# Row maxima of a 64 MB matrix: tail rows turned by TensorE and reduced by GpSimd, other load sizes, and a moved store

## The chip, the cores and the metric

The kernel runs on one core of one Trainium2 chip. The metric is the device time of one execution in microseconds (us), as the median of several runs. TensorE is written PE in the profile, VectorE DVE, ScalarE ACT, GpSimd POOL and SyncE SP.

## The reference

The input x has shape (32, 512, 1024) in 32-bit floats, which is 67.1 MB. The output is the maximum over the last axis, shape (32, 512):

```python
def reference(x):
    return np.max(x, axis=-1).astype(np.float32)
```

Seen by the kernel, x is a matrix of 16384 rows with 1024 columns, and one number is wanted for each row.

## The kernel before

The rows are spread over the 128 partitions, so each partition holds 128 rows of 1024 columns. In what follows "a row" is one such row in every partition: 128 rows of x, 512 KB. The rows come in two blocks. The first has 112 rows in 15 loads, from 14 rows down to 3, the second 16 rows in 11 loads of two rows and one. In a block of S rows, partition p holds the S rows from p times S on, so each partition reads one piece of consecutive memory per load, and its results leave as one piece as well.

The loop of lines 41 to 55 does three things. For each load, SP issues a DMA from x into a ring of 46 rows in SBUF (line 49; a load that would pass the end of the ring starts at its beginning again, line 47). For each load, VectorE takes the maximum over the columns of all its rows in a single reduction into columns of the tile `res` (line 50). At the end of each block, ACT issues the store of the block's columns of `res` (line 54).

No order is written out by hand. The framework gives each engine its instructions in the order of the loop and adds waits on semaphores. A reduction waits for its load. A load waits for the reductions of the rows whose place in the ring it takes. The DMAs of both queues, SP's and ACT's, take eight semaphores in turn, and a DMA that takes a semaphore again waits for the landing of the DMA that had it before. TensorE, and apart from four start-up constants GpSimd, do nothing.

Of the kernel before, what the change touches and what calls it, by code (L numbers as in the profile page):

```python
# [1 line left out]

# [4 lines left out]


F32 = mybir.dt.float32

BLOCKS = [
    [14, 14, 12, 11, 9, 8, 8, 7, 6, 5, 4, 4, 4, 3, 3],
    [2, 2, 2, 2, 2, 1, 1, 1, 1, 1, 1],
]
RING = 46


@with_exitstack  # L20
def kernel(
    ctx: ExitStack,
    tc: tile.TileContext,
    x: bass.AP,
    out: bass.AP,
):
    nc = tc.nc
    P = 128
    X = mybir.AxisListType.X

    xf = x.flatten_outer_dims()
    N, D = xf.shape
    I = N // P
    of = out.flatten_outer_dims()

    once = ctx.enter_context(tc.tile_pool(name="once", bufs=1))
    ring = once.tile([P, RING, D], F32)
    res = once.tile([P, I], F32)

    at = first = 0  # L40
    for loads in BLOCKS:
        S = sum(loads)
        xb = xf[first * P:(first + S) * P, :].rearrange("(p i) d -> p i d", p=P)
        b = 0
        for g in loads:
            if at + g > RING:
                at = 0
            xc = ring[:, at:at + g, :]
            nc.sync.dma_start(out=xc, in_=xb[:, b:b + g, :])  # L49
            nc.vector.reduce_max(out=res[:, first + b:first + b + g], in_=xc, axis=X)  # L50
            at += g
            b += g
        dst = bass.AP(tensor=of.tensor, offset=of.offset + first * P, ap=[[S, P], [1, S]])
        nc.scalar.dma_start(out=dst, in_=res[:, first:first + S])
        first += S
    assert first == I


# [1 line left out]
_INS = ['x']  # L60
_OUTS = [((32, 512), 'float32')]


# [23 lines left out]
```

## Time and profile before

| | |
|---|---|
| Median of 9 runs | 165.09 us (165.04 to 165.26) |
| The profiled execution | 165.26 us, of which the span is 163.5 us |
| VectorE busy | 138.5 us, 26 reductions |
| Loads on SP's queue | 26 DMAs, 67.11 MB, 96.3% of the span's DMA time |
| Stores on ACT's queue | 2 DMAs, 0.07 MB, 0.2% |
| VectorE idle ahead of a load | 22.5 us in four waits, the longest 20.3 us, at the start |

The span runs from the first to the last instruction of the program in one profiled execution. The page gives busy times for each engine, the span in 40 slices with the busy share in tenths, the DMA queues, the chain of work that ended last, and groups of equal instructions with their mean duration and the idle time just ahead of them. Other answers of the trace give the chain in order of time and, for each engine or queue, what it waited for.

### The profile page before, as it was taken

What the parts mean: (1) busy time and instruction counts of PE and PEld (TensorE: products, weight loads), DVE (VectorE), ACT (ScalarE), POOL (GpSimd) and SP (SyncE); (2) the same over time, 40 slices, a digit from 0 to 9 for tenths busy, and PEclk for the clock granted to TensorE, in tenths of its full rate; (3) what the DMA queues carried; (4) which work ended last, traced back from release to release, by engine and by line L of the source; (5) the groups of instructions that cost most, each with busy time, mean ns of one, the idle gap of its engine ahead of it and who ended that gap; (6) DMA issues with size and microseconds to landing.
All of it is one profiled execution on the core that took longest, in us unless ns stands there. A gap on an engine that the chain in (4) does not pass through costs nothing.

```text
span 163.5 us, 109 instructions
## 1 busy us (share of the span) xinstructions
DVE 138.5 (85%) x26; POOL 0.2 (0%) x4
## 2 busy tenths in 40 slices
DVE  0000099968999999999999999999999999999994
POOL 0000000000000000000000000000000000000000
DMA  6999999999899897999999999999999999999980
GB/s 224 449 449 449 449 449 449 449 405 397 385 445 485 353 518 332 433 433 489 425 393 489 401 442 442 399 425 436 418 425 425 433 416 422 423 420 417 406 337 2
DMA packets 4032, 67.18 MB, mean 411 GB/s; under 512 B 704, under 2 KB 704, under 8 KB 1472
## 3 DMA queue, kind: packets, MB, share of 16 engines
q1 hardware_dynamic: 3744, 67.11, 96.3%
q10 hardware_dynamic: 288, 0.07, 0.2%
HBM read 67.11 MB, written 0.07 MB: 411 GB/s over the span
## 4 chain that ended last, share of the span: by engine, by line
DMA 57%; DVE 40%; DVEq 1%; SPq 0%; issue 0%
DMA ring<-in_x_dram 57%; DVE res L50 40%; DVEq L82 1%; SPq L49 0%
## 5 line engine op out<-in xcount | busy, mean ns | idle before, releaser
L50 DVE TENSOR_REDUCE res<-ring 128x1 f32<-128x1024 f32 (+11 forms) x26 | 138.5, 5398 | 22.5 <-DMA ring<-in_x_dram 22.5
L71 POOL MEMSET const-bfloat16-1.0<- 128x1 bf16 x1 | 0.1, 101 | 0.0
L71 POOL MEMSET const-uint8-127<- 128x1 uint8 x1 | 0.1, 101 | 0.0
L71 POOL MEMSET const-float32-0.0<- 128x1 f32 x1 | 0.1, 98 | 0.2 <-issue 0.2
L71 POOL MEMSET const-float32-1.0<- 128x1 f32 x1 | 0.1, 98 | 0.0
## 6 DMA issues: line engine op xcount, KB each, us to landing
ring<-in_x_dram SPq DMA_DIRECT2D x2, 7168.0 KB, 27.8
ring<-in_x_dram SPq DMA_DIRECT2D x2, 4096.0 KB, 31.6
ring<-in_x_dram SPq DMA_DIRECT2D x1, 6144.0 KB, 50.1
ring<-in_x_dram SPq DMA_DIRECT2D x3, 2048.0 KB, 36.8
ring<-in_x_dram SPq DMA_DIRECT2D x1, 5632.0 KB, 29.6
ring<-in_x_dram SPq DMA_DIRECT2D x5, 1024.0 KB, 24.6
ring<-in_x_dram SPq DMA_DIRECT2D x1, 4608.0 KB, 23.6
ring<-in_x_dram SPq DMA_DIRECT2D x1, 3584.0 KB, 38.3
```

What stands on the lines that cost most here:

```text
L50: nc.vector.reduce_max(out=res[:, first + b:first + b + g], in_=xc, axis=X)
L71: nc = _bacc.Bacc("TRN2", target_bir_lowering=False, num_devices=1)
L82: with _tile.TileContext(nc) as tc:
```

## The change

The change has five parts.

1. The loads: the first block's 112 rows come in 10 loads (15, 15, 15, 13, 13, 11, 9, 9, 6, 6), the second block's first 15 rows in 10 (3, 3, 2 and seven single rows).
2. The last row comes in two loads of 512 columns, the second into a tile of its own, `tail`. VectorE writes the first half's maximum into the column of `tail` just ahead of the second half and then reduces 513 columns. With these there are 22 loads.
3. The first block's store is issued after both loops and waits for the reduction of the last full row, the 20th load's. The second block's store follows on the same queue.
4. One row of the 9th load, three of the 10th and one of the 13th are not reduced by VectorE. For each, TensorE transposes the eight squares of 128 by 128 into PSUM (`turn`), ACT copies the 128x1024 result to SBUF, and GpSimd takes the maximum over the 128 partitions with `partition_all_reduce`, which writes it to every partition. TensorE then turns the first partition's 1024 numbers back in eight pieces (`back`), so that each partition holds the eight maxima of its row's eight column groups, and VectorE reduces these eight into `res`. These merging reductions stand behind the reductions of the 10th, 16th and 19th load.
5. VectorE builds an identity matrix at the start, in eight small instructions, and its instructions and TensorE's are held in a written order by `in_turn`.

On TensorE the order is: turn and way back of the 9th load's row; three turns and the first way back of the 10th load's rows; the turn of the 13th load's row; and then the remaining three ways back. GpSimd also gets one instruction ahead of the first all-reduce, which selects its library, and ACT one that loads its function table.

The core of the diff:

```diff
 BLOCKS = [
-    [14, 14, 12, 11, 9, 8, 8, 7, 6, 5, 4, 4, 4, 3, 3],
-    [2, 2, 2, 2, 2, 1, 1, 1, 1, 1, 1],
+    [15, 15, 15, 13, 13, 11, 9, 9, 6, 6],
+    [3, 3, 2, 1, 1, 1, 1, 1, 1, 1],
 ]
 RING = 46
+TENSOR = {
+    8: [("turn", 8, 0), ("back", 8, 0)],
+    9: [("turn", 9, 0), ("turn", 9, 1), ("turn", 9, 2), ("back", 9, 0)],
+    12: [("turn", 12, 0), ("back", 9, 1), ("back", 9, 2), ("back", 12, 0)],
+}
+BY_GPSIMD = {8: 1, 9: 3, 12: 1}
+MERGE = {9: 8, 15: 9, 18: 12}
...
+    turned = ctx.enter_context(tc.tile_pool(name="turned", bufs=2))
+    allr = ctx.enter_context(tc.tile_pool(name="allr", bufs=2))
+    psum = ctx.enter_context(tc.tile_pool(name="psum", bufs=3, space=bass.MemoryType.PSUM))
+    psmall = ctx.enter_context(tc.tile_pool(name="psmall", bufs=2, space=bass.MemoryType.PSUM))
...
+    def turn(j, k):
+        rows, cols = tiles[j]
+        ps = psum.tile([P, D], F32)
+        for c in range(C):
+            in_turn("PE", nc.tensor.transpose(
+                out=ps[:, c * P:(c + 1) * P],
+                in_=rows[:, k, c * P:(c + 1) * P],
+                identity=ident,
+            ))
+        sb = turned.tile([P, D], F32)
+        nc.scalar.copy(out=sb, in_=ps)
+        top = allr.tile([P, D], F32)
+        nc.gpsimd.partition_all_reduce(top, sb, P, bass_isa.ReduceOp.max)
+        tops[j, k] = top
+
+    def back(j, k):
+        if j not in backs:
+            fetched = psmall.tile([P, BY_GPSIMD[j], C], F32)
+            backs[j] = fetched
+        for c in range(C):
+            in_turn("PE", nc.tensor.transpose(
+                out=backs[j][:, k, c:c + 1],
+                in_=tops[j, k][0:1, c * P:(c + 1) * P],
+                identity=ident[0:1, 0:1],
+            ))
...
-            nc.vector.reduce_max(out=res[:, first + b:first + b + g], in_=xc, axis=X)
+            cols = res[:, first + b:first + b + n]
+            m = BY_GPSIMD.get(j, 0)
+            tiles[j] = xc[:, n - m:, :], cols[:, n - m:]
+            for what, i, k in TENSOR.get(j, []):
+                (turn if what == "turn" else back)(i, k)
+            reduce = in_turn("DVE", nc.vector.reduce_max(
+                out=cols[:, :n - m], in_=xc[:, :n - m, :], axis=X))
+            if j in MERGE:
+                i = MERGE[j]
+                in_turn("DVE", nc.vector.reduce_max(out=tiles[i][1], in_=backs[i], axis=X))
...
-        nc.scalar.dma_start(out=dst, in_=res[:, first:first + S])
...
+    half = ring[:, at, :H]
+    nc.sync.dma_start(out=half, in_=xb[:, b, :H])
+    nc.sync.dma_start(out=tail[:, PAD:], in_=xb[:, b, H:])
+    in_turn("DVE", nc.vector.reduce_max(out=tail[:, PAD - 1:PAD], in_=half, axis=X))
+    in_turn("DVE", nc.vector.reduce_max(out=res[:, I - 1:], in_=tail[:, PAD - 1:], axis=X))
+    store = nc.scalar.dma_start(out=views[0][0], in_=views[0][1])
+    tc.add_manual_dep(store.ins, reduce.ins.name, SYNC, reason="behind the loads")
+    nc.scalar.dma_start(out=views[1][0], in_=views[1][1])
```

## The prediction

> **What bounds the kernel now.** I read the page first (busy shares, slices, chain), then the chain in order of time, the groups by shape, SP's own waits, and the DMA issues. Times inside the run are microseconds from the span's start; landings of single loads are read from the trace's landing records.
>
> ```profile
> DVE 138.5 (85%) x26; POOL 0.2 (0%) x4
> ...
> DVE  0000099968999999999999999999999999999994
> ...
> GB/s 224 449 449 449 449 449 449 449 405 397 385 445 485 353 518 332 433 433 489 425 393 489 401 442 442 399 425 436 418 425 425 433 416 422 423 420 417 406 337 2
> ...
> DMA ring<-in_x_dram 57%; DVE res L50 40%; DVEq L82 1%; SPq L49 0%
> ```
>
> The loads never stop (about 420 GB/s up to the last slices) and VectorE is full from the seventh slice on: two engines of almost the same pace. The chain shows how they hand over:
>
> ```profile
> 1.15 36.07 DMA ring<-in_x_dram
> 37.22 0.02 issue
> 37.25 58.00 DVE res L50 x5
> ...
> 132.04 19.94 DMA ring<-in_x_dram
> 151.97 0.02 issue
> 152.00 7.92 DVE res L50 x6
> 159.91 1.13 DVEq L82
> ```
>
> VectorE waits for a load at 37.2, a little at 95.4, and last at 152.0 (0.17). The last load lands at 159.61; VectorE, 0.23 late, ends its last row at 161.05, the last store goes out at 161.08 and lands at 162.50, and 1.0 of closing follows to 163.49. The pace of each is in the next lines and in the landings:
>
> ```profile
> L50 DVE TENSOR_REDUCE res<-ring 128x14 f32<-128x14336 f32 x2 | 30.2, 15086 | 22.2 <-DMA ring<-in_x_dram 22.2
> L50 DVE TENSOR_REDUCE res<-ring 128x2 f32<-128x2048 f32 x5 | 11.2, 2283 | 0.2 <-DMA ring<-in_x_dram 0.2
> L50 DVE TENSOR_REDUCE res<-ring 128x1 f32<-128x1024 f32 x6 | 6.8, 1208 | 0.0
> L50 DVE TENSOR_REDUCE res<-ring 128x3 f32<-128x3072 f32 x2 | 6.6, 3349 | 0.0
> ```
>
> From 15086 for 14 rows and 1208 for one (a row is 1024 columns), a reduction costs 0.141 + 1.067 n us; started back to back, the spacing is 0.057 + 1.067 n (a three-row one starts 3.26 before its successor, a one-row one 1.125). Landings follow 1.203 n + 0.07: 16.92 for 14 rows, 8.50 for 7, 1.27 for one. So a row costs VectorE 0.14 less than the DMA, and each load costs the DMA 0.07 more.
>
> ```profile
> SPq L49 <- DVE res L50: 77.6, 7, 15.1
> SPq L49 <- DMA ring<-in_x_dram: 56.6, 10, 18.3
> ...
> SPq L49 <- DMA out_dram<-res: 5.0, 1, 5.0
> ```
>
> The last line matters for the moved store: SP stood 5.0 us on the first block's store, because the load behind it reuses that store's semaphore. It was harmless: loads issued from 149.8 on land 8.6 us or more later, behind a full queue.
>
> ```profile
> out_dram<-res ACTq DMA_DIRECT2D x1, 56.0 KB, 6.7
> out_dram<-res ACTq DMA_DIRECT2D x1, 8.0 KB, 1.4
> ```
>
> **What the Trainium skill says.** "DMA: Bandwidth & Descriptors", Issuing engines are not separate DMA queues: all queues share 16 engines and interleave. The trace agrees: the 56 KB store took 6.7 us among loads, the 8 KB one 1.4 alone; the two-row load beside the store took 2.66 against 2.45 to 2.50 for its neighbours. "SBUF — State Buffer", Who interferes with whom: `tensor_reduce` never contends with GpSimd on this chip; no instruction here shows it. "GPSIMD Engine Reference", 3.1: a tight one-input loop runs at about 1.8 cycles per element, a two-input one at 2.6, at 1.2 GHz; section 3.2 there knows only a partition-axis `tensor_reduce` of 128x2048, 247.7 us. No run here shows GpSimd computing. The same page, 2.1: the first call of a freshly loaded kernel pays about 6 us. Not shown here either.
>
> **The change part by part.**
>
> *22 loads for 26, 15 15 15 13 13 11 9 9 6 6, then 3 3 2, seven single rows, two halves.* With the landing rule the loads land at 21.6, 39.7, 57.8, 73.6, 89.3, 102.6, 113.5, 124.4, 131.6, 138.9, 142.6, 146.3, 148.8, then every 1.28 to 157.8, the halves at 158.4 and 159.1. That is 0.5 sooner than 159.61: four loads at 0.07, and the store's 0.2 out of the way. SP issues four DMAs fewer; ring waits now stand before 4th, 5th, 6th, 8th, 9th and 12th load, each released when a reduction ends at least 15 us before the load queued just ahead has landed (tightest: the sixth load waits for the third reduction, 73.9, with the fifth landing at 89.3), so the queue stays full; the last loads wait for the landing eight loads back, some 10 us ahead. The waits cost nothing.
>
> *VectorE's work.* Summed with the spacing rule it waits last at 89.3, for the fifth load, and then never again: 13, 11, 9, 9 rows to 134.3, five of the ninth load to 139.7, three of the tenth to 142.97, the first merge, 3 and 3, one of the thirteenth load to 150.8, single rows with a merge behind the 16th and 19th load, and the twentieth load's row to 158.99. The three merges read 8 or 24 numbers from PSUM; the fixed 0.14 of a reduction bounds them below, 0.3 above; I take 0.17 each, 0.5 in all. Five rows leave VectorE: 5 x 1.067 = 5.3. They pay for the larger loads, whose wait for the fifth landing comes at 89.3 with 57 rows still to do, where before the last wait came at 152.0. So this is now a VectorE-bound tail whose every delay reaches the end.
>
> *The last row in halves.* Half a row is 0.53 + 0.14 = 0.67. The first half starts behind the row before at 158.99 (it landed at 158.4) and takes its 0.59 of spacing; the second has to wait for the first's result, so the usual overlap of 0.08 with its end is lost (I take 0.1), and it runs its full 0.67: 160.35. Before: 161.05. The gain is 0.70.
>
> *The first store* now waits for VectorE at 158.99. ACT needs about 0.4 to issue it and is free before 160.38, when the last store goes out; its packets follow about 0.9 later, past the last landing at 159.1. An empty queue took 1.4 for the small store, so it lands near 160.6 to 161.3, before the last store (160.38 + 1.42 = 161.8). No load stands behind it any more, and it is hidden; if it were not, at most 0.5.
>
> *The identity.* Eight small VectorE instructions before the first reduction. VectorE stands idle for 20.3 us there in the trace before, 21.6 now. At the price of a reduction of 128 columns, 0.14 + 0.13, an estimate of 0.3 each, they take under 3. Hidden. The table load on ACT and GpSimd's library at the start are hidden likewise, unless their transfers delay the first loads: none to 0.3, I take 0.
>
> *The five turned rows* are the disputed part: eight transposes, a PSUM copy on ACT, an all-reduce on GpSimd, eight transposes back, then the merge on VectorE, which is in order: all reductions queued behind a merge wait with it. Prices: "TensorE: Matmul & The Clock Gate", Part 4, gives 275 to 390 ns for one transpose, so eight are at most 3.1; pipelined I take 2.0, and 0.7 back (from one partition). The copy is 0.186 + 1024 x 0.83 ns = 1.04 by "ScalarE: Activation LUTs", What ACT_TABLE_LOAD costs. With a for one all-reduce: the first merge is ready at 131.64 + 2.0 + 1.05 + a + 0.7 = 135.39 + a, needed at 142.97: a up to 7.6. The three rows of the tenth load stand on TensorE behind the first row's way back; so their merge is ready at 135.39 + a + 3.05 + 3a + 0.7 = 139.14 + 4a, needed at 154.15: a up to 3.75. The last is behind all five: 139.14 + 5a, needed at 157.69: a up to 3.71. Past that the end is 141.80 + 5a: each further microsecond costs five.
>
> What is a? Per column a core has to fold on the way in and write on the way back. Two passes of a tight loop: 2 x 1.8 x 1024 / 1.2 GHz = 3.07. Two passes at the two-input rate: 4.44. With a reduction over 16 lanes in software on one core, some eight more operations a column at three a cycle, 2.3 more: 6.7. The ends are 1.8 (two passes at one cycle) and 124 (half of the page's other instruction, which isn't this one). I take 3.07 and no wait; the margin is 0.64, thin.
>
> *Sum.* 161.05 becomes 160.35, and what follows (store, closing) is the same. The profiled execution took 165.26 with a span of 163.5, 1.8 outside it; it becomes 164.56. It lies 0.17 above the median of nine, 165.09, so the forecast is 164.4.
>
> **The rivals.**
>
> *GpSimd becomes the bound* (the other side). Decides from a = 3.71, at the merges behind the 16th and 19th load. At a = 4.44: 141.80 + 22.2 = 164.0, 3.65 later than 160.35: 168.0. At 6.7: 175.3, so 179.3. For it: nothing in the profile shows GpSimd cheap, and the page's rates straddle the limit. Against: only the tightest loop is needed.
>
> *The first all-reduce pays its library load*, 6 us at 134.7: first merge 1.4 late, the second again 1.4; 167.2. Against: an idle GpSimd can load in the first 130 us.
>
> *TensorE is the slow one*: above 3.2 us for eight transposes, the two turns and copies of the tenth load push its merge past 154.15; at 4 us, 4.3 late, 168.7.
>
> *The gain is eaten*: start-up transfers on the DMA rings delay loads by some 0.5 before 89.3, and all of it reaches the end; 164.9 to 165.2.
>
> **How the numbers follow.** Forecast case 0.50 (164.0 to 164.9: merges 0.14 to 0.3, start-up to 0.3). Gain eaten 0.06. Library load or slow TensorE 0.08. GpSimd bound with a from 3.7 to 5: 0.18 (164.6 to 170.8); with a above 5: 0.18, up to 180 and beyond. The range from 164.0 to 173.0 leaves out most of the last case and some edges. Measured runs spread by 0.13%, so 0.2% (0.33 us) is about what can be told from no change. Faster 0.50, same 0.06, slower 0.44.
>
> **What would show it.** Right: VectorE's last wait for a load near 89.3; no wait on PE before the merges; the last reduction ending near 160.3; five GpSimd starts that follow the data, with nothing over 3.7 between two of the tenth load's. Wrong: waits of the merge line for PE or GpSimd, VectorE's slices below 9 from the 35th on, and GpSimd starts back to back: then a is their spacing, and the end should follow 141.80 + 5a. If VectorE waits for loads after 89.3, the landing rule failed.

## The result and the profile after

The changed kernel takes 164.41 us (median of 9 runs, 164.21 to 164.56), the kernel before 165.10 us (29 runs). The ratio is 0.9956, 95% interval [0.9948, 0.9965]: 0.7 us or 0.4% faster. The forecast was 164.4.

The profiled execution of the changed kernel has a span of 162.7 us, 0.8 less than before. Its page, busy time of each engine and VectorE's row of 40 slices; then the shares of the chain:

```profile
PE 13.0 (8%) x80; PEld 11.7 (7%) x80; DVE 135.0 (83%) x33; ACT 6.3 (4%) x6; POOL 16.3 (10%) x9
...
DVE  3000079995999779999996999999999999999994
...
DMA 63%; DVE 34%; SPq 0%; issue 0%
```

GpSimd, idle before, works for 16.3. VectorE is full to the end, as before, in spite of five rows less. The chain in order of time shows where the two paces meet now:

```profile
89.25 25.82 DVE res L139 x2
...
115.09 31.28 DMA ring<-in_x_dram
...
146.40 7.86 DVE res L139 x5
```

The last wait that the prediction expected, at 89.25, is there. But from 115 on the chain runs once more through the loads, up to the 12th load's landing at 146.38, which VectorE meets at 146.40. Before, the last hand-over from loads to VectorE was at 152.0. A later meeting leaves no idle time and so is not in the chain: the 20th load lands at 157.84, and VectorE starts on it at 157.86.

GpSimd's all-reduces in order of time (start, length, what, in brackets the idle time before it and what ended it):

```profile
134.87 3.22 POOL L106 PARTITION_ALL_REDUCE top<-sb  x1 [134.44 <-ACT sb L104]
142.19 9.63 POOL L106 PARTITION_ALL_REDUCE top<-sb  x3 [4.10 <-ACT sb L104]
152.10 3.22 POOL L106 PARTITION_ALL_REDUCE top<-sb  x1 [0.27 <-ACT sb L104]
```

TensorE from the first way back on, in the same form:

```profile
138.14 1.01 PE L115 MATMUL fetched<-ident,top 1*128 1x1 f32 x8 [4.42 <-POOL top L106]
...
148.96 1.94 PE L98 MATMUL ps<-ident,ring 128*128 128x128 f32 x8 [2.66 <-issue]
150.83 2.06 PE L115 MATMUL fetched<-ident,top 1*128 1x1 f32 x16
155.38 1.01 PE L115 MATMUL fetched<-ident,top 1*128 1x1 f32 x8 [2.49 <-POOL top L106]
```

An all-reduce takes 3.22, three in a row 9.63. The ways back for the three merges end at 139.15, 152.89 and 156.39. VectorE's side shows what they meet:

```profile
142.96 0.15 DVE L143 TENSOR_REDUCE res<-fetched 128x1 f32<-128x8 f32 x1
...
154.18 0.17 DVE L143 TENSOR_REDUCE res<-fetched 128x3 f32<-128x24 f32 x1
...
157.71 0.16 DVE L143 TENSOR_REDUCE res<-fetched 128x1 f32<-128x8 f32 x1
157.86 1.22 DVE L139 TENSOR_REDUCE res<-ring 128x1 f32<-128x1024 f32 x1
...
159.71 0.69 DVE L156 TENSOR_REDUCE res<-tail 128x1 f32<-128x513 f32 x1
```

No merge carries idle time in brackets. The merges stand at 142.96, 154.18 and 157.71, so they had 3.8, 1.3 and 1.3 to spare. The last reduction ends at 160.40 (161.04 before). The last load landed at 159.15 (159.61 before), and the last store at 161.85 (162.49 before). What follows that landing took 0.83 instead of 0.99, which makes the span 0.80 shorter and not 0.64.

### The profile page after: what moved, and what is told of

Same layout as the page of the kernel before. It is cut to its first block, busy times and chain, and to the rows that moved or that the text cites. A ratio compares the mean times of both kernels' runs of the same rounds, so it can differ in the third digit from the quotient of the medians.

```text
span 162.7 us, 293 instructions
## 1 busy us (share of the span) xinstructions
PE 13.0 (8%) x80; PEld 11.7 (7%) x80; DVE 135.0 (83%) x33; ACT 6.3 (4%) x6; POOL 16.3 (10%) x9
## 4 chain that ended last, share of the span: by engine, by line
DMA 63%; DVE 34%; SPq 0%; issue 0%
DMA ring<-in_x_dram 63%; DVE res L139 34%; DVE res L156 0%; DVE tail L155 0%; SPq L133 0%; DVE res L143 0%
## 5 line engine op out<-in xcount | busy, mean ns | idle before, releaser
L139 DVE TENSOR_REDUCE res<-ring 128x1 f32<-128x1024 f32 (+6 forms) x20 | 132.1, 6653 | 24.4 <-DMA ring<-in_x_dram 24.4
L106 POOL PARTITION_ALL_REDUCE top<-sb x5 | 16.1, 3253 | 138.8 <-ACT sb L104 138.8
L98 PE MATMUL ps<-ident,ring 128*128 128x128 f32 x40 | 8.3, 388 | 134.4 <-DMA ring<-in_x_dram 131.8
L98 PEld LDWEIGHTS ps<-ident,ring 128*128 128x128 f32 x40 | 7.3, 208 | 134.5 <-issue 134.5
L104 ACT COPY sb<-ps 128x1024 f32<-128x1024 f32 x5 | 5.1, 1012 | 144.9 <-PE ps L98 143.2
L115 PE MATMUL fetched<-ident,top 1*128 1x1 f32 x40 | 4.9, 238 | 8.9 <-POOL top L106 8.9
L115 PEld LDWEIGHTS fetched<-ident,top 1*128 1x128 f32 x40 | 4.4, 206 | 10.1 <-POOL top L106 9.6
L156 DVE TENSOR_REDUCE res<-tail 128x1 f32<-128x513 f32 x1 | 0.7, 687 | 0.0
L155 DVE TENSOR_REDUCE tail<-ring 128x1 f32<-128x512 f32 x1 | 0.7, 677 | 0.0
L143 DVE TENSOR_REDUCE res<-fetched 128x1 f32<-128x8 f32 (+1 forms) x3 | 0.5, 161 | 0.0
```

The source lines that it names most:

```text
L98: in_turn("PE", nc.tensor.transpose(out=ps[:, c * P:(c + 1) * P], in_=rows[:, k, c * P:(c + 1) * P], identity=ident,))
L104: nc.scalar.copy(out=sb, in_=ps)
L106: nc.gpsimd.partition_all_reduce(top, sb, P, bass_isa.ReduceOp.max)
L115: in_turn("PE", nc.tensor.transpose(out=backs[j][:, k, c:c + 1], in_=tops[j, k][0:1, c * P:(c + 1) * P], identity=ident[0:1, 0:1],))
L139: reduce = in_turn("DVE", nc.vector.reduce_max(out=cols[:, :n - m], in_=xc[:, :n - m, :], axis=X))
L143: in_turn("DVE", nc.vector.reduce_max(out=tiles[i][1], in_=backs[i], axis=X))
```

## The experiments

In a profile, the first landing of different executions lies up to 0.3 apart with the same loads (21.25 to 21.53 among the runs that begin with three loads of 15 rows), so small differences are taken from the timed runs.

### The parts one by one

**The moved store alone**, on the kernel before:

```diff
-        nc.scalar.dma_start(out=dst, in_=res[:, first:first + S])
+        views.append((dst, res[:, first:first + S]))
...
+    store = nc.scalar.dma_start(out=views[0][0], in_=views[0][1])
+    tc.add_manual_dep(store.ins, reduces[-2].ins.name, SYNC, reason="behind the loads")
+    nc.scalar.dma_start(out=views[1][0], in_=views[1][1])
```

> The kernel before with only the first block's store moved behind the reduction of the next-to-last load. Theory (VectorE and the loads are balanced at the end, and VectorE's last wait, 0.17 at 152.0, is for a load that the store held up by 0.17 to 0.2): the wait shrinks by that much, VectorE's end comes 0.15 to 0.2 sooner, 164.9. Rival (the store is hidden by the full queue, since VectorE is 0.2 late at the end anyway): 165.1, no change. Rival (the store at the end delays the closing): later than 165.1.

164.98 us, ratio 0.9993 [0.9985, 1.0001]. That is 0.09 faster, half of what the theory asked for, and the interval reaches to no change: at most 0.25 us comes from here. In its trace VectorE still meets the 20th load:

```profile
151.71 0.02 issue
151.73 7.92 DVE res L52 x6
```

Its wait there is 0.11 instead of 0.17, so it has shrunk by 0.06 and not by the theory's 0.15 to 0.2. The 56 KB store lands in 1.6 behind the loads instead of 6.7 among them.

**The last row in halves alone**, on the kernel before, with two loads of 512 columns and the two chained reductions of the change:

> The kernel before with only the last row in two loads of 512 columns, chained. Theory (VectorE reaches the last row 0.23 after it has landed, so the split only adds VectorE's fixed time, one start and the wait of the second half for the first): 0.15 to 0.2 later, 165.25. Rival (the point of the split: after the last landing only half a row, 0.67 instead of 1.21, is left): 0.5 sooner, 164.6.

165.33 us, ratio 1.0016 [1.001, 1.0023]: slower. The end of its chain in order of time:

```profile
151.87 7.74 DVE res L52 x6
...
159.71 0.69 DVE tail L61
...
160.42 0.69 DVE res L62
```

The two halves stand back to back on VectorE; neither waits for its load. What the split hides was not exposed, and VectorE pays a fixed time and a start more.

**The last row whole**, in the changed kernel:

```diff
-    nc.sync.dma_start(out=half, in_=xb[:, b, :H])
-    nc.sync.dma_start(out=tail[:, PAD:], in_=xb[:, b, H:])
-    in_turn("DVE", nc.vector.reduce_max(out=tail[:, PAD - 1:PAD], in_=half, axis=X))
-    in_turn("DVE", nc.vector.reduce_max(out=res[:, I - 1:], in_=tail[:, PAD - 1:], axis=X))
+    nc.sync.dma_start(out=whole, in_=xb[:, b:b + 1, :])
+    in_turn("DVE", nc.vector.reduce_max(out=res[:, I - 1:], in_=whole, axis=X))
```

> The changed kernel with the last row in one load and one reduction, 21 loads. Theory (VectorE reaches the first half 0.5 after its landing; the split costs VectorE 0.16 more than it saves after the landing, or nothing): between 0.15 sooner and 0.05 later than the changed kernel, 164.3. Rival (the split is worth the half row that it hides, 0.5): 164.9.

164.32 us, ratio 0.9954 [0.9942, 0.9967], the same as the changed kernel. The halves give nothing there either.

**The store back among the loads**, in the changed kernel (the dependence on the 20th load's reduction left out):

> The changed kernel without the wait of the first block's store for the 20th load's reduction: it goes out when the block's last merge is done, near 154.4, among the last loads. Theory (the store takes about 0.18 of the engines' time from the loads, which VectorE now reaches within 0.1 of their landing): 0.1 to 0.2 later than the changed kernel, 164.55. Rival (VectorE's lag hides it): 164.4.

164.32 us, ratio 0.9951 [0.9937, 0.9964]. The rival was right. The store went out at 154.18 and took 5.1 to land. Only the gap before the last half's landing grew, from 0.64 to 0.75, and VectorE reached that half 0.45 after its landing anyway. So in the changed kernel the store's place is worth nothing that can be measured.

**The new loads without the turned rows** (TENSOR, BY_GPSIMD and MERGE empty):

> The changed kernel with its loads, halves and moved store, but no row turned: VectorE reduces all 128 rows, the identity stays. Theory (VectorE is full from the fifth load on, so five rows at 1.067 come back and three merges at 0.09 go): 5.1 later, 169.5. Rival (the loads alone set the end, as the last one lands at 159.2 in either case): 164.4 to 165.

169.16 us, ratio 1.0245 [1.0229, 1.026]. The loads land as early as in the changed kernel (the last at 159.19), but from the fifth load on the chain is VectorE alone, which ends at 165.12:

```profile
89.15 70.08 DVE res L134 x12
```

**The turned rows without the new loads**: the 26 loads of before, the last row whole, the store moved, four rows turned.

```diff
+BY_GPSIMD = {12: 1, 13: 1, 14: 1, 15: 1}
+MERGE = {14: 12, 16: 13, 17: 14, 19: 15}
```

> The kernel before with its 26 loads and the last row whole, the moved store, and four rows turned, one each of the 13th to 16th load. Theory (the turned rows only pay by allowing the larger, fewer loads; with the old ones VectorE waits for landings instead): as with the moved store alone, 165.0, 0.1 to either side, with VectorE busy 4 less and waiting 4 more. Rival (the turned rows themselves give the gain, four of them 0.5 or more): 164.5 or less.

165.18 us, ratio 1.0009 [1.0001, 1.0018]; no gain, even 0.2 more than with the moved store alone. The four rows' time became waits, here from VectorE's order of time:

```profile
139.32 2.29 DVE L141 TENSOR_REDUCE res<-ring 128x2 f32<-128x2048 f32 x1 [1.40 <-DMA ring<-in_x_dram]
...
144.29 2.29 DVE L141 TENSOR_REDUCE res<-ring 128x2 f32<-128x2048 f32 x1 [1.26 <-DMA ring<-in_x_dram]
...
151.76 2.29 DVE L141 TENSOR_REDUCE res<-ring 128x2 f32<-128x2048 f32 x1 [0.22 <-DMA ring<-in_x_dram]
```

(VectorE's busy time fell from 138.5 to 136.6 only, as the identity and the merges are in it.) At 151.76 it is where the kernel with only the store moved was, 151.73. So neither the new loads alone nor turned rows beside the old loads give anything; together they give the 0.7. (The second run has four turned rows, not the same five.)

### Where the limit lies

**A sixth row turned**, a second one of the ninth load:

```diff
-    8: [("turn", 8, 0), ("back", 8, 0)],
-    9: [("turn", 9, 0), ("turn", 9, 1), ("turn", 9, 2), ("back", 9, 0)],
+    8: [("turn", 8, 0), ("turn", 8, 1), ("back", 8, 0)],
+    9: [("turn", 9, 0), ("back", 8, 1), ("turn", 9, 1), ("turn", 9, 2), ("back", 9, 0)],
...
-BY_GPSIMD = {8: 1, 9: 3, 12: 1}
+BY_GPSIMD = {8: 2, 9: 3, 12: 1}
-MERGE = {9: 8, 15: 9, 18: 12}
+MERGE = {10: 8, 15: 9, 18: 12}
```

> The changed kernel with a sixth row turned, a second one of the ninth load, its merge behind the 11th load. Theory (from the 12th load on VectorE and the loads run level, so a row fewer before that only makes VectorE wait for landings): 164.3 to 164.5, with new waits of VectorE for loads before 146.4. Rival (VectorE alone is full from 89.3 on, as the prediction has it): 0.5 sooner, 163.9, down to the last landing plus half a row.

164.30 us, ratio 0.9953 [0.994, 0.9965], the same as with five. VectorE's order of time shows the row's time come back as waits for loads, 0.32, 0.34 and, at 146.24, 0.25:

```profile
138.87 3.35 DVE L139 TENSOR_REDUCE res<-ring 128x3 f32<-128x3072 f32 x1 [0.32 <-DMA ring<-in_x_dram]
142.56 3.35 DVE L139 TENSOR_REDUCE res<-ring 128x3 f32<-128x3072 f32 x1 [0.34 <-DMA ring<-in_x_dram]
```

From the 12th load on the kernel runs at the pace of the landings and of VectorE at once: in the changed kernel too, VectorE starts on the 12th and on the 20th load 0.02 after they land.

**Every all-reduce done twice**, into the same tile:

```diff
         nc.gpsimd.partition_all_reduce(top, sb, P, bass_isa.ReduceOp.max)
+        nc.gpsimd.partition_all_reduce(top, sb, P, bass_isa.ReduceOp.max)
```

> The changed kernel with every all-reduce done twice into the same tile (the result is the same), so one row costs GpSimd 6.4 instead of 3.2. Theory (past 3.71 the end follows 141.80 + 5a, as five all-reduces then stand in a row and VectorE waits at the merges): end near 173.8 in the span, 177 to 179 in all, with VectorE idle for 11 to 12 at the merge behind the 16th load and 2 to 3 at the one behind the 19th. Rival (VectorE and the loads set the end, GpSimd lies beside them): 164.4.

179.19 us, ratio 1.0856 [1.0836, 1.0875]. VectorE now waits at both later merges, as its order of time says:

```profile
165.88 0.18 DVE L144 TENSOR_REDUCE res<-fetched 128x3 f32<-128x24 f32 x1 [11.70 <-PE fetched L116]
...
172.41 0.17 DVE L144 TENSOR_REDUCE res<-fetched 128x1 f32<-128x8 f32 x1 [2.96 <-PE fetched L116]
```

The first pair takes 6.53, and the last two pairs start 6.52 apart (the pairs of the tenth load's first two rows run interleaved); 141.80 + 5 x 6.52 = 174.4, and the last reduction ended at 175.01.

**One all-reduce more**, the first row of the tenth load's done twice:

> The changed kernel with one more all-reduce, the first row of the tenth load's done twice. Theory (the second merge is ready 1.3 before VectorE needs it, the third likewise, so of 3.2 more on GpSimd 1.9 comes out): 166.3, the wait at the merge behind the 16th load. Rival (GpSimd stands idle for 4.1 before the tenth load's rows and has room for one more): 164.4. Rival (no slack): 167.6.

166.29 us, ratio 1.0075 [1.0062, 1.0089], 1.9 over the changed kernel, with one wait of 1.96 at the second merge. So its slack was 3.2 less 1.9, the 1.3 read from the trace; the 4.1 that GpSimd idles before 142.19 can't be used by what arrives later.

**The transposes done twice**:

```diff
-        for c in range(C):
+        for c in [*range(C), *range(C)]:
             in_turn("PE", nc.tensor.transpose(
                 out=ps[:, c * P:(c + 1) * P],
```

> The changed kernel with the eight transposes of each turn done twice on TensorE (same result). In the trace of the changed kernel they start 0.21 apart, and 0.11 apart from 142.3 on, after some 3 of work without a gap. Theory (TensorE has room too: the second merge was ready 1.3 early; the extra 24 transposes of the tenth load's rows run mostly at 0.11): 1.5 to 2.5 later, 166.3. Rival (they keep 0.21): 168.9. Rival (TensorE lies beside the path): 164.4.

166.24 us, ratio 1.007 [1.0056, 1.0083]. The 48 transposes of the tenth load's rows took 7.06, not 48 x 0.21 = 10.1, and the second merge waited 1.95. But the faster pace is not why the loss is small, as GpSimd's order of time shows:

```profile
136.42 3.22 POOL L106 PARTITION_ALL_REDUCE top<-sb  x1 [136.00 <-ACT sb L104]
145.34 12.84 POOL L106 PARTITION_ALL_REDUCE top<-sb  x4 [5.70 <-ACT sb L104]
```

From 145.34 on GpSimd works without a pause. Counted from the first landing, that start is 3.33 later than in the changed kernel: two groups of eight more transposes lie in front of it, the first turned row's and the tenth load's first row's, and all of these ran 0.21 apart; they cost 1.7 and 1.6. Less the slack of 1.3, 2.0 remain. The faster transposes come after 144.04, and most of their time lies beside all-reduces for which the later rows have to wait anyway. By an estimate from these starts, 0.21 throughout would have made the second merge about 0.5 later still, far from the rival's 168.9. So the number came as the theory said, but mostly not for its reason.

### Fewer loads still

**20 loads, the last row whole**, blocks of 113 and 15 rows:

```diff
-    [15, 15, 15, 13, 13, 11, 9, 9, 6, 6],
-    [3, 3, 2, 1, 1, 1, 1, 1, 1, 1],
+    [15, 15, 15, 14, 13, 10, 9, 9, 8, 5],
+    [3, 3, 2, 1, 1, 1, 1, 1, 1],
```

> The changed kernel with the last row whole and 20 loads, 15 15 15 14 13 10 9 9 8 5, then 3 3 2 and seven single rows, five rows turned as before. Theory (after the 12th load the landings set the end, each load costs 0.065 of fixed time, and two loads fewer than 22 are two such times, the split's cost on VectorE gone as well): 0.1 to 0.2 sooner than the changed kernel, 164.25. Rival (the merges, now with 0.3 of slack, come late): 164.6 or more.

164.66 us, ratio 0.9977 [0.9967, 0.9986]: a miss, and not by the rival's cause, since no merge waits. VectorE ended at 160.20, as planned. The loss lies behind that, in the last store; its line of the DMA issues (KB, us from issue to landing):

```profile
out_dram<-res ACTq DMA_DIRECT2D x1, 7.5 KB, 2.1
```

The second store, 60 bytes per partition, took 0.7 longer here than the 64-byte ones. But this execution is the slowest of its ten, 165.11 against 164.52 to 164.81 for the other nine, so the 0.7 isn't typical.

**20 loads with blocks of 112 and 16**, as a test of that:

```diff
+    [15, 15, 15, 14, 13, 10, 9, 9, 8, 4],
+    [4, 3, 2, 1, 1, 1, 1, 1, 1],
...
+BY_GPSIMD = {8: 1, 9: 2, 11: 1, 12: 1}
+MERGE = {9: 8, 12: 9, 16: 11, 18: 12}
```

> The last row whole and 20 loads as in the run before with 20, but with the blocks at 112 and 16 rows again: 15 15 15 14 13 10 9 9 8 4, then 4 3 2 and seven single rows, five rows turned: one of the 9th load, two of the 10th, one each of the 12th and 13th. Theory (that run lost 0.7 after its last reduction, whose store of 60 bytes per partition took 2.1 from issue to landing instead of 1.4; with 64 bytes it is 1.4 again, and two loads fewer are worth 0.1 to 0.2): 164.25. Rival (the fewer, larger loads cost it, not the store): 164.6 or more.

164.34 us, ratio 0.9947 [0.9934, 0.9961]. The same line:

```profile
out_dram<-res ACTq DMA_DIRECT2D x1, 8.0 KB, 1.4
```

The loss is gone with the 60-byte rows. VectorE's end is 160.15 here and 160.20 there, so in the profiled execution the loss lay in the store. Between the medians it is 0.3; whether the store makes this up as well isn't shown, as no other execution of that kernel was profiled. Against the changed kernel with its 22 loads the gain can't be told from none. None of the variants that kept pace (164.30 to 164.34) is measurably below 164.41.

## Why the prediction was right, step by step

| Step | Predicted | Measured |
|---|---|---|
| First, fifth, last landing | 21.6, 89.3, 159.1 | 21.49, 89.23, 159.15 |
| Eight transposes; copy | 2.0; 1.05 | 1.94; 1.01 |
| One all-reduce, a | 3.07 (1.8 to 124) | 3.22 |
| Eight transposes back | 0.7 | 0.83 to 1.01 |
| Merges ready (predicted: its sums with a = 3.07) | 138.5, 151.4, 154.5 | 139.15, 152.89, 156.39 |
| Merges needed | 142.97, 154.15, 157.69 | 142.96, 154.18, 157.71 |
| Merge on VectorE | 0.17 | 0.07 to 0.09 of its path |
| Last reduction ends | 160.35 | 160.40 |
| Median | 164.4 | 164.41 |

*The disputed size.* The whole forecast hung on a lying below 3.71. 3.22 us for 1024 columns is, by an estimate with the 1.2 GHz of the Trainium skill's "GPSIMD Engine Reference", 3.1, 3.8 cycles a column, near two passes of that section's tight loop (3.6); that the instruction makes two such passes no run shows. The choice was right and had been given a chance of one half; the page alone could not settle it, so the hit is in part luck. Doing one more (1.9 slower) and doing all twice (14.8 slower) show both the threshold and the slope of about five that the rival stated. The rival was real; only its size didn't occur. The rival with a slow TensorE is of the same kind: doubling the transposes cost 1.8. The library load didn't show: the first all-reduce, at 134.87, took 3.22 like the others.

*The margin.* It was thinner than the 0.64 stated: the slack at the second and third merge was 1.3, not 2.7 and 3.2. A part of this is a mistake in the sums, which let the chain of turns run on without waiting for its loads. They start the tenth load's rows at 135.39 + 3.07 = 138.46, before that load's landing at 138.9 in the prediction's own list, and they put the last merge behind five all-reduces, at 154.5, although its row lands only at 148.8, which with the same prices makes 155.6. With the landings the stated prices leave 2.3 and 2.1. The rest is prices: the ways back took 1.0 instead of 0.7, and each all-reduce 0.15 more. So a could have been some 0.3 larger, no more.

*What pays.* The prediction said that the five rows pay for the larger loads. The two runs that took one without the other show it: new loads alone 4.1 slower than before, turned rows alone no gain. The run without the halves and the one without the moved store each kept the 0.7. The sum is short: the last landing came 0.46 sooner, and VectorE's distance from it fell from 1.43 to 1.25, which is the 0.64 at the end of the last reduction. That the median meets the forecast to 0.01 is luck: VectorE ended 0.05 later than forecast, the time after the last store's landing was 0.16 shorter, and the profiled execution lay 0.05 above the median, where 0.17 had been taken.

*What was wrong.* Besides the margin two statements didn't hold, though neither moved the sum. First, "this is now a VectorE-bound tail": VectorE is no more alone in it than before. A sixth row turned changes nothing, as the loads' landings are as late as VectorE. The prediction's own numbers had this: they put the 12th load's landing at 146.3 and VectorE's start on it at 146.40, and for the 20th load 157.8 and, with the merge in front of it, 157.86. The part that does hold, that a delay of VectorE reaches the end, is shown by the waits at the merges. Second, the step on the halves gave the 0.70 as if the split were its source; the split gives nothing in the changed kernel and costs 0.2 in the kernel before. The store, put at 0.2 for the landings, is worth about 0.1 before, not clear of nothing, and nothing after. The one cost put at nothing that could have been more, the start-up of identity, table and library, was nothing: the first landing is at 21.49, and 20.30 before plus the 1.20 of one row more is 21.50. Two smaller slips: at 89.3 there are 70 rows left and not 57, which leaves out the fifth load's own, and 65 of them are VectorE's; and with 6 us for a library load the prediction's sums make the end 3.3 later and not 2.8.

What stays open: the 0.2 by which the run with turned rows and old loads lies over the one with the moved store alone. Its merge behind the 20th load takes 0.07 of VectorE's path where no slack is left. In the profiles the time after the last store's landing is 0.1 longer as well (1.09 against 0.99); whether that is so in other executions isn't shown. Open too is how few turned rows would do: only none, five and six were run with the new loads.

## What to carry to other kernels

Where two engines run level, work taken off one of them turns into its waiting time; it pays only if it is spent at once on what slows the other, here on fewer and larger loads. Work sent round over three other engines must be costed as a chain, with the landings that it waits for, ending at a strictly ordered engine: read when each result is ready and when it is needed, and double one link at a time to learn the slack, looking in the trace for where the added time lies. Splitting the last piece helps only if the engine that takes it is waiting for it.

## What the runs showed of the hardware

- An all-reduce over 128 partitions of 1024 floats takes 3.22 us on GpSimd, and 3.22 to 3.30 in every run here; back to back they start 3.1 to 3.3 apart. No first call of a run was longer. VectorE's three-row reductions took 3.34 to 3.35 with GpSimd at work beside them, as in the kernel before without it (3.35).
- Transposes of 128x128 floats start 0.21 apart. The 275 to 390 ns that the Trainium skill's "TensorE: Matmul & The Clock Gate", Part 4, gives are for one of bf16 from start to end; the records here are 0.39 long on average, with modelled ends, and overlap. In five of the ten runs with turned rows the spacing fell to 0.11, in the changed kernel at 142.34, 3.3 into an unbroken row of them, in others up to 4.3 into it. With all all-reduces doubled, 24 in a row took 5.38 without such a change. In the changed kernel the spacing was 0.21 again at 148.96, after a pause of 2.66; the granted clock had been 1.00 up to 142.3 and was 0.50 by then, so which of the two matters isn't shown.
- A store with rows of 60 bytes for each partition took 2.1 us from issue to landing in the one execution profiled, its kernel's slowest, with rows of 64 bytes 1.4. Between the medians of the two kernels with 20 loads lie 0.3 us.
